# Low halves of some MLP weights by an accumulating DMA instead of a VectorE subtraction

## The chip, the cores and the metric

The kernel runs on one core of a Trainium2 chip. The metric is device time in microseconds (us): the median over the timed runs of the program. A verdict compares two kernels run on the same chip, with a 95% interval.

The core has five engines with instruction queues of their own: TensorE (PE, with its weight loads shown as PEld), VectorE (DVE), ScalarE (ACT), GpSimd (POOL) and SyncE (SP), which here only issues DMAs. The profile numbers the DMA queues: q1 carries what SP issues, q0 what POOL issues; both run on the same 16 DMA engines.

## The reference, cut to what matters

A two-layer decoder trunk over 256 tokens of width 2048, in float32. Layer 0 has a gated short convolution, layer 1 latent attention; both end in an MLP with a hidden width of 8192, followed by a layer norm:

```python
def sq_relu_mlp(x, w1, w2):
    return jnp.square(jax.nn.relu(x @ w1)) @ w2
...
        h = layer_norm(ALPHA * h + sq_relu_mlp(h, mlp_w1[layer], mlp_w2[layer]),
                       ln_g[layer, 1], ln_b[layer, 1])
```

The two MLPs are where the change acts. W1 is 2048 x 8192 and W2 is 8192 x 2048 in each layer.

## The kernel before, in words

**Numbers in two parts.** Matrix products are made in TensorE's fp32r format. To keep float32's accuracy every weight tile is split into a high part, the tile rounded to fp32r, and a low part, what is left over. `split` (L109) does that with two instructions: ACT copies `raw` into `hi` with the rounding (L111), and the DVE subtracts, `lo = raw - hi` (L112). Activations are split likewise, so that a product becomes high by high, high by low and low by high (L190, L194 and `dot`, L245).

**The stream of weights.** All weights are cut into half units, each [128, 1024] in float32, 512 KB. `stream` (L64 to L83) lists them in the order of their use. `take` (L171) hands the next ones to the code that multiplies, and first calls `prepare` (L135) for units up to `LOOK` = 5 ahead. `prepare` loads a unit from HBM on SP's queue (`load_raw`, L130, issue at L132) into one of `RAW` = 5 raw buffers and splits it into a `hi` and a `lo` tile, of which there are `WA` = 8 each (`parts`, L117).

**Who waits for whom.** A load waits for a raw buffer; the buffer is free when the instructions that read it are done. A high part waits for its load and for a `hi` buffer, which is free when PE has used the unit that lies eight back. The low part waits for the high part. No order is written by hand: the framework's scheduler sets the order of each engine's queue when the program is built, from the order of the code and from when it expects an instruction's inputs and buffers to be free. At run time each queue works strictly in that order, so an instruction that waits holds all behind it.

**A pass of an MLP.** The hidden width is worked in `NQ` = 8 passes of 1024 (`mlp`, L523). In each pass:

- W1: eight output tiles of 128 hidden columns, each from two half units, which hold the first and the second 1024 of the contraction (`products`, L230, `mm_run`, L196). In pass 0 these products are made by `mm_wide` (L217) with the layer norm folded in, in passes 1 to 7 by `mm_run`: for each of 16 blocks of the contraction one matmul of 512 columns with the high part (L190) and one of 256 with the low part (L194). The result is evacuated by `whole` (L300: ACT copies one half at L303, the DVE adds the other at L304), goes through ReLU and square on ACT (L562, L563) and is split into `h` (L308, L309).
- Fast W2: in passes 1 to 6 of the first MLP and 1 to 7 of the second (`FAST`, 13 passes in all) the first two of W2's four column blocks are multiplied by a scheme with 7 products instead of 8 (`down_fast`, L287; its matmuls write `ps_f`). Its units, w2f, come in pairs of half units. For each pair the DVE makes a third raw tile, `raw_t`, in a raw buffer (L154), two combinations of half the size (L157, L160), and after three splits a fourth small one, `t` (L162, also through L111 and L112). A pair costs three `hi` and `lo` buffers. Left operands made of `h` stand in `forms` (L566 to L574).
- Plain W2: the other column blocks by `down` (L259; `ps_d`). Results are added into `acc` by the DVE (L546).

**Other users.** POOL has little to do: memsets for the convolution (L507) and for `kpe` (L655), and four loads of the last norm's vectors, `gbt` (L869), at the end of the second MLP.

**Lines that the prediction names.** L111 and L112: the split. L132: the issue of a weight load. L154: the third raw tile of a w2f pair. L190 and L194: high and low matmuls of W1. L247: first matmul of `dot`. L303, L304, L562: evacuation of a W1 product. L869: `gbt`.

Of the kernel before, what the change touches and what calls it, by code (L numbers as in the profile page):

```python
# [9 lines left out]
F32 = mybir.dt.float32  # L10
F32R = mybir.dt.float32r
AF = mybir.ActivationFunctionType
ALU = mybir.AluOpType
# [9 lines left out]
QC = FF // NQ // P  # L23
# [22 lines left out]
def trunk(ctx: ExitStack, tc: tile.TileContext, xT, vecs, w_in, w_out, w_kv, w_q, w_uk, w_uv,  # L46
          w_qn, w_qp, w_o, w1, w2, w2f, cosT, sinT, mask, ident, gb, out):
    nc = tc.nc
# [10 lines left out]
    def halves(w):  # L59

        lead = len(w.shape) - 2
        return [(w,)] if lead == 0 else [h for i in range(w.shape[0]) for h in halves(w[i])]

    stream = []  # L64
# [1 line left out]
        stream += halves(w_in[NC + m]) + halves(w_in[2 * NC + m]) + halves(w_in[m])  # L66
    stream += halves(w_out)

    def mlp_stream(l):
        out = []  # L70
        for q in range(NQ):
            out += halves(w1[l, q * QC:(q + 1) * QC])
            lead = 0
            if q in FAST[l]:
                out += [(w2f[l, q, j, 0], w2f[l, q, j, 1]) for j in range(QC // 2)]
                lead = 2
            out += halves(w2[l, q, lead:])
        return out

    stream += mlp_stream(0) + halves(w_kv) + halves(w_q)  # L80
    for g in range(4):
        stream += halves(w_uk[g]) + halves(w_qn[g]) + halves(w_uv[g]) + halves(w_qp[g])
    stream += halves(w_o) + mlp_stream(1)  # L83

    class Banks:

# [22 lines left out]
    def split(hi, lo, src):  # L109

        nc.scalar.copy(hi, src)  # L111
        nc.vector.tensor_tensor(lo, src, hi.bitcast(F32), ALU.subtract)  # L112

    def tiled(w):
        return w.rearrange("p (b c) -> p b c", c=P)

    def parts(i):  # L117
        return tuple(whl.tile([P, 8, P], F32R, tag=t, name=f"{t}{i}") for t in ("hi", "lo"))
# [11 lines left out]
    def load_raw(i, src):  # L130
        raw = raws.tile([P, 1024], F32, tag="raw", name=f"raw{i}")
        nc.sync.dma_start(raw, src)  # L132
        return raw

    def prepare(i):  # L135

        if len(stream[i]) == 1:
            raw = load_raw(i, stream[i][0])
            hi, lo = ready[i] = parts(i)
            split(hi, lo, tiled(raw))  # L140
            return
        r1, r2 = (load_raw(f"{i}_{j}", src) for j, src in enumerate(stream[i]))
        out = []

        def finished(r, name):
            hi, lo = parts(name)
            split(hi, lo, tiled(r))
            out.append((hi, lo))

        b22, (b21, b12) = r1[:, BW:], (r2[:, :BW], r2[:, BW:])  # L150
        finished(r1, f"{i}_1")
        t = raws.tile([P, 1024], F32, tag="raw", name=f"raw{i}_t")
        two = "p (a c) -> p a c"
        nc.vector.tensor_tensor(t.rearrange(two, a=2), b12.unsqueeze(1).to_broadcast([P, 2, BW]),  # L154
                                r1.rearrange(two, a=2), ALU.subtract)
        finished(t, f"{i}_t")
        nc.vector.tensor_tensor(b12, b22, t[:, :BW], ALU.subtract)  # L157
        finished(r2, f"{i}_2")
        t4 = r1[:, :BW]
        nc.vector.tensor_tensor(t4, b21, b12, ALU.subtract)  # L160
        f = state["fast"].tile([P, 2, BW], F32R, tag="t4", name=f"t4_{i}")
        split(f[:, 0, :], f[:, 1, :], t4)  # L162
        b1, t13, b2 = ([[v.rearrange("p b c -> p (b c)")[:, o:o + BW] for v in w] for o in (0, BW)] for w in out)
        ready[i] = {"11": b1[0], "22": b1[1], "21": b2[0], "T2": b2[1], "T1": t13[0], "T3": t13[1],
                    "T4": [f[:, 0, :], f[:, 1, :]]}
# [5 lines left out]
    def take(halves=2):  # L171

        i = state["next"]
        state["next"] += halves
        ahead = -sum(size(j) for j in range(i, i + halves))
        for j in range(i, len(stream)):
            ahead += size(j)
            if ahead > LOOK:
                break
            if j >= state["split"]:  # L180
                prepare(j)
                state["split"] = j + 1
        return [ready.pop(i + j) for j in range(halves)]
# [295 lines left out]
    for half, cuts in enumerate(FIRST):  # L479
        pieces = [load(2 * u + half, first[:, GROUP * half + u, :], cuts) for u in range(GROUP)]  # L480
        for b0, b1 in zip(cuts, cuts[1:]):
            at = slice(8 * half + b0, 8 * half + b1)
# [502 lines left out]
```

## Time and profile before

| | us |
|---|---|
| median of the two timed runs | 2053.64 (2053.06 and 2054.22) |
| span of the profiled execution, first to last instruction | 2049.4 |
| what lies outside the span, by the difference | 4.2 |
| PE busy | 2030.6 |
| DVE busy | 1662.8 |
| ACT busy | 1194.1 |
| POOL busy | 4.5 |

How to read the profile. A group line gives source line, engine and operation, `out<-in` by the program's tile names, the shape, the count, then busy time, mean of one in ns, and the engine's idle time just before these instructions with what ended it. A line of the timeline gives start, duration, engine, line, operation, tiles, shape and count, and in brackets the idle time before it with its releaser. A row of the windows view gives a stretch in us from the span's start, then the busy time of PE, PEld, DVE, ACT and POOL with instruction counts, the granted clock of TensorE, the mean busy share of the 16 DMA engines, and what they moved in GB/s. A line of the waits view gives who waited for whom, the total, the number of waits and the longest. A DMA issue line gives the queue's engine, the count, the size of one and the median time from issue to landing. Matmuls overlap, so their single durations are longer than their distance.

One pass takes 86.5 us. In the pass that the prediction follows, PE works on W1 from 631.7 to 676.9; its first w2f matmul starts at 676.9.

### The profile page before, as it was taken

What the parts mean: (1) busy time and instruction counts of PE and PEld (TensorE: products, weight loads), DVE (VectorE), ACT (ScalarE), POOL (GpSimd) and SP (SyncE); (2) the same over time, 40 slices, a digit from 0 to 9 for tenths busy, and PEclk for the clock granted to TensorE, in tenths of its full rate; (3) what the DMA queues carried; (4) which work ended last, traced back from release to release, by engine and by line L of the source; (5) the groups of instructions that cost most, each with busy time, mean ns of one, the idle gap of its engine ahead of it and who ended that gap; (6) DMA issues with size and microseconds to landing.
All of it is one profiled execution on the core that took longest, in us unless ns stands there. A gap on an engine that the chain in (4) does not pass through costs nothing.

```text
span 2049.4 us, 30194 instructions
## 1 busy us (share of the span) xinstructions
PE 2030.6 (99%) x11208; PEld 1760.4 (86%) x11208; DVE 1662.8 (81%) x2602; ACT 1194.1 (58%) x1860; POOL 4.5 (0%) x25
## 2 busy tenths in 40 slices
PE   9999999999999999999999999999999999999997
PEld 8888888988888888888889998898888888888885
DVE  7667677678898988989788878776879888898988
ACT  6444445676566565655656665566656656566562
POOL 0000000000000000000000000000000000000000
PEclk9999999999999999999999999999999999999998
DMA  8666666564746557465755544656475664756653
GB/s 308 202 188 187 186 185 194 159 211 136 249 142 223 193 167 250 143 226 173 234 169 164 166 124 142 197 174 196 138 236 161 196 218 156 243 153 217 212 165 137
DMA packets 108003, 385.32 MB, mean 188 GB/s; under 512 B 11984, under 2 KB 13392, under 8 KB 107856
## 3 DMA queue, kind: packets, MB, share of 16 engines
q1 hardware_dynamic: 107136, 381.04, 58.7%
q0 software_dynamic: 576, 2.10, 0.3%
q8 instruction: 88, 1.44, 0.3%
q14 instruction: 59, 0.48, 0.1%
q10 hardware_dynamic: 144, 0.26, 0.0%
HBM read 381.25 MB, written 2.10 MB: 187 GB/s over the span
## 4 chain that ended last, share of the span: by engine, by line
PE 97%; DVE 1%; DMA 1%; issue 0%; ACT 0%; SPq 0%; DVEq 0%
PE ps_u L190 34%; PE ps_u L194 17%; PE ps_d L248 7%; PE ps_d L247 7%; PE ps_d L249 7%; PE ps_f L249 4%; PE ps_f L248 4%; PE ps_f L247 4%; PE ps_w L224 1%; PE ps_w L222 1%; PE ps_w L223 1%; PE ps_g L222 1%; PE ps_g L224 1%; PE ps_g L223 1%; PE ps_wo L190 1%; PE S L788 1%
## 5 line engine op out<-in xcount | busy, mean ns | idle before, releaser
L112 DVE TENSOR_TENSOR lo<-raw,hi 128x1024 fp32r<-128x1024 f32 x712 | 861.7, 1221 | 299.0 <-ACT hi L111 294.3
L111 ACT CAST hi<-raw 128x1024 fp32r<-128x1024 f32 x712 | 742.2, 1049 | 526.6 <-PE ps_u L190 289.5
L190 PE MATMUL ps_u<-xhl,hi 128*128 128x512 f32 x1792 | 632.2, 398 | 0.0
L194 PE MATMUL ps_u<-xhl,lo 128*128 128x256 f32 x1792 | 503.0, 281 | 0.0
L190 PEld LDWEIGHTS ps_u<-xhl,hi 128*128 128x128 f32 x1792 | 336.5, 188 | 82.3
L194 PEld LDWEIGHTS ps_u<-xhl,lo 128*128 128x128 f32 x1792 | 338.5, 189 | 0.5
L190 PE MATMUL ps_u<-xhl_a,hi 128*128 128x512 f32 x720 | 253.4, 396 | 0.0
L248 PE MATMUL ps_d<-lo,h 128*128 128x512 f32 x608 | 236.9, 390 | 0.0
L249 PE MATMUL ps_d<-hi,h 128*128 128x512 f32 x608 | 236.8, 390 | 0.0
L247 PE MATMUL ps_d<-hi,h 128*128 128x512 f32 x608 | 236.6, 389 | 0.0
L194 PE MATMUL ps_u<-xhl_a,lo 128*128 128x256 f32 x720 | 202.9, 282 | 0.0
L190 PEld LDWEIGHTS ps_u<-xhl_a,hi 128*128 128x128 f32 x720 | 135.2, 188 | 31.9
L194 PEld LDWEIGHTS ps_u<-xhl_a,lo 128*128 128x128 f32 x720 | 135.8, 189 | 0.0
L248 PEld LDWEIGHTS ps_d<-lo,h 128*128 128x128 f32 x608 | 114.1, 188 | 24.2 <-DVE lo L112 0.4
L247 PEld LDWEIGHTS ps_d<-hi,h 128*128 128x128 f32 x608 | 114.2, 188 | 24.0
L249 PEld LDWEIGHTS ps_d<-hi,h 128*128 128x128 f32 x608 | 114.1, 188 | 23.9
L111 ACT CAST hi_t<-raw_t 128x1024 fp32r<-128x1024 f32 x52 | 54.8, 1054 | 77.8 <-PE ps_u L190 41.8
L190 PE MATMUL ps_u<-z,hi 128*128 128x512 f32 x256 | 89.0, 392 | 0.0
L562 ACT ACTIVATE fh<-fh 128x256 f32<-128x256 f32 x112 | 46.4, 414 | 72.0 <-DVE fh L304 72.0
L222 PE MATMUL ps_w<-xd,hi 128*128 128x258 f32 x256 | 72.5, 284 | 0.0
L224 PE MATMUL ps_w<-xd,hi 128*128 128x258 f32 x256 | 72.5, 285 | 0.0
L223 PE MATMUL ps_w<-xd,lo 128*128 128x258 f32 x256 | 72.3, 282 | 0.0
(235 smaller groups left out, 3254.8 us busy)
## 6 DMA issues: line engine op xcount, KB each, us to landing
raw<-in_w_dram SPq DMA_DIRECT2D x408, 512.0 KB, 4.4
raw<-in_w2f_dram SPq DMA_DIRECT2D x104, 512.0 KB, 3.6
raw<-in_w_in_dram SPq DMA_DIRECT2D x90, 512.0 KB, 4.2
raw<-in_w_out_dram SPq DMA_DIRECT2D x32, 512.0 KB, 3.6
raw<-in_w_o_dram SPq DMA_DIRECT2D x32, 512.0 KB, 3.9
raw<-in_w_kv_dram SPq DMA_DIRECT2D x10, 512.0 KB, 4.3
raw<-in_w_q_dram SPq DMA_DIRECT2D x8, 512.0 KB, 4.5
raw<-in_w_uk_dram SPq DMA_DIRECT2D x8, 512.0 KB, 4.4
```

What stands on the lines that cost most here:

```text
L111: nc.scalar.copy(hi, src)
L112: nc.vector.tensor_tensor(lo, src, hi.bitcast(F32), ALU.subtract)
L190: nc.tensor.matmul(ps, w[blk // 8][0][:, blk % 8, :], x, start=first, stop=False)
L194: nc.tensor.matmul(ps[:, :T], w[blk // 8][1][:, blk % 8, :], x[:, :T], start=False, stop=last)
L222: nc.tensor.matmul(ps[:, :W], hi, x[k][:, :W], start=k == 0, stop=False)
L223: nc.tensor.matmul(ps[:, :W], lo, x[k][:, :W], start=False, stop=False)
L224: nc.tensor.matmul(ps[:, :W], hi, x[k][:, W:], start=False, stop=k == NC - 1)
L247: nc.tensor.matmul(ps, x[0], w[0], start=first, stop=False)
L248: nc.tensor.matmul(ps, x[0], w[1], start=False, stop=False)
L249: nc.tensor.matmul(ps, x[1], w[0], start=False, stop=last)
L562: nc.scalar.activation(f, f, AF.Relu)
L788: nc.tensor.matmul(S[:, at:at + n], qp[:, tok], kp[:, :n], start=False, stop=True)
```

## The change

For each second half unit of W1 in passes 1 to 7 of both MLPs (8 units a pass, 112 in all) the low part is made in another way. ACT copies the high part as before. ACT then writes its negative into the `lo` tile, an activation with the function Copy and scale -1. Then POOL issues a DMA from the raw tile to the `lo` tile, both in SBUF, that adds to what is there: `lo = -hi + raw`. The DVE instruction at L112 is no longer made for these units. All other units, among them the first halves of the same W1 tiles, all of pass 0, W2 and the attention's weights, are split as before. `summed_lo` holds the places of the changed units in the stream: `mlp_stream` is given the length of the stream so far and notes every second one of a pass's sixteen W1 units.

```diff
+    summed_lo = set()
+
-    def mlp_stream(l):
+    def mlp_stream(l, at):
         out = []
         for q in range(NQ):
+            if q > 0:
+                summed_lo.update(range(at + len(out) + 1, at + len(out) + 2 * QC, 2))
             out += halves(w1[l, q * QC:(q + 1) * QC])
...
-    stream += mlp_stream(0) + halves(w_kv) + halves(w_q)
+    stream += mlp_stream(0, len(stream))
+    stream += halves(w_kv) + halves(w_q)
...
-    stream += halves(w_o) + mlp_stream(1)
+    stream += halves(w_o)
+    stream += mlp_stream(1, len(stream))
...
             hi, lo = ready[i] = parts(i)
-            split(hi, lo, tiled(raw))
+            if i in summed_lo:
+                nc.scalar.copy(hi, tiled(raw))
+                nc.scalar.activation(lo, hi.bitcast(F32), AF.Copy, scale=-1.0)
+                nc.gpsimd.dma_start(lo, tiled(raw), accum_op=ALU.add)
+            else:
+                split(hi, lo, tiled(raw))
             return
```

## The prediction

> **What bounds the kernel now.** I read the page first (busy shares, clock, queues, chain), then the groups by line, then one middle pass of the MLP by windows, waits and timeline.
>
> ```profile
> span 2049.4 us, 30194 instructions
> PE 2030.6 (99%) x11208; PEld 1760.4 (86%) x11208; DVE 1662.8 (81%) x2602; ACT 1194.1 (58%) x1860; POOL 4.5 (0%) x25
> q1 hardware_dynamic: 107136, 381.04, 58.7%
> q0 software_dynamic: 576, 2.10, 0.3%
> PE 97%; DVE 1%; DMA 1%; issue 0%; ACT 0%; SPq 0%; DVEq 0%
> L112 DVE TENSOR_TENSOR lo<-raw,hi 128x1024 fp32r<-128x1024 f32 x712 | 861.7, 1221 | 299.0 <-ACT hi L111 294.3
> L111 ACT CAST hi<-raw 128x1024 fp32r<-128x1024 f32 x712 | 742.2, 1049 | 526.6 <-PE ps_u L190 289.5
> raw<-in_w_dram SPq DMA_DIRECT2D x408, 512.0 KB, 4.4
> raw<-in_w2f_dram SPq DMA_DIRECT2D x104, 512.0 KB, 3.6
> ```
>
> PE is busy for 99% of the span and is 97% of the chain that ended last. Only 18.8 us are open to anyone, so a gain of 2% (41 us, about what a measurement of this kernel can tell from no change) is out of reach unless matmuls themselves get shorter, and the change touches none. The question is whether it makes PE wait.
>
> The stage where it acts is a pass of the MLP. I take pass 3 of the first layer: W1 from 631.7 to 676.9, then the fast w2f units and the plain w2 units. Rows of the windows view (PE, PEld, DVE, ACT, POOL busy, clock, DMA share, GB/s):
>
> ```profile
> 545.20:631.70 86.50, 86.50 (x437) 73.08 (x436) 74.78 (x104) 52.19 (x78) 0.00 (x0) 1.00 0.61 194
> 631.70:676.90 45.20, 45.20 (x257) 39.21 (x256) 38.10 (x59) 28.88 (x49) 0.00 (x0) 1.00 0.55 172
> 617.40:643.10 25.70, 25.70 (x129) 21.72 (x128) 22.09 (x25) 13.95 (x17) 0.00 (x0) 1.00 0.90 303
> 664.00:695.00 31.00, 31.00 (x153) 25.89 (x152) 30.02 (x44) 19.89 (x32) 0.00 (x0) 1.00 0.49 149
> 625.00:630.00 5.00, 5.00 (x24) 4.14 (x23) 4.58 (x5) 3.16 (x3) 0.00 (x0) 1.00 1.00 375
> ```
>
> The clock is full, so nothing there can move. The 16 loads of the pass's W1 units run in a burst (617.4 to 643.1) that fills the DMA engines to 0.90. The DVE is nearly full (30.02 of 31.0) while it prepares the w2f units. Those two places are where slack is short.
>
> **The change part by part.** *DVE loses* 112 subtractions (8 second halves, 7 passes, 2 layers) of 1.22 us: 137 us, or 9.8 us per pass. PE did not wait for them, so this is worth nothing by itself; below it pays back part of a delay.
>
> *ACT gains* 112 negations. Their form, one 128x1024 input written as fp32r, is that of the cast at 1.05 us: 118 us, 8.4 us per pass. In the W1 stage ACT then has 28.9 + 8.4 = 37.3 of 45.2 us. The cover is its idle time, less what it spends waiting for the DVE:
>
> ```profile
> ACT fh L562 <- DVE fh L304: 4.6, 4, 1.4
> ```
>
> That makes 41.9 of 45.2, so I count zero; without the cover each pass loses what exceeds 45.2.
>
> *POOL gains* 112 issues. The only ones in this trace are those of gbt:
>
> ```profile
> L869 POOL DMA_DIRECT2D gbt<-in_gb_dram x4: 527/529/664, 1991.0 to 1992.7; - x4
> DMA to landing us min/median/max: 4.6/5.8/9.4
> ```
>
> At 0.53 us each that is 59 us on an engine with 4.5 us of work; nothing else is queued there in these passes but the memset of kpe and the gbt issues, which already wait until W1 of the last pass is done. A POOL issue waits for ACT's negation, and what queues behind it is only the next accumulation, 5.7 us of PE time later. Zero.
>
> *The DMA engines gain* 112 accumulations of 512 KB that read raw and lo and write lo. No row shows one. From below: as dear as a copy. At a share of 1.00 the engines move 375 GB/s, so 512 KB take 1.40 us of all sixteen (q0's four gbt loads: 0.3% of 2049.4 us over 4, 1.5 us). From above: both reads in full, 2.80 us, if the adder costs nothing; beyond that see the rivals. I take 2.3 us, nearer to the double than to the copy, since the second read is certain and only what a packet pays besides reading can be shared. Over the span q1's loads hold 58.7%, in this pass 0.61 of 86.5 us, so 33.7 us are free and 8 x 2.3 = 18.4 us fit on average. It is not the average that matters.
>
> *Two waits change.* First, the low part of a second half is ready later. Nearest to its use is the first second half of a pass:
>
> ```profile
> 623.60 1.05 ACT L111 CAST hi<-raw 128x1024 fp32r<-128x1024 f32 x1 [1.45 <-DMA raw<-in_w_dram]
> 634.77 0.28 PE L194 MATMUL ps_u<-xhl,lo 128*128 128x256 f32 x1
> ```
>
> High part done at 624.65, negation at 625.7, landing 5.8 + (2.3 - 1.4) = 6.7 us on: 632.4, and PE wants it at 634.8. Zero, with 2.4 us in hand; at the longest landing (9.4 + 1.4) it would be 1.7 us late, 24 us over 14 passes.
>
> Second, the raw buffer stays held until the accumulation has landed, and SP's queue waits for it. Each w2f load waits for such a buffer. The tightest is the one that follows the pass's last W1 unit:
>
> ```profile
> 642.76 0.33 SPq L132 DMA_DIRECT2D raw<-in_w_dram  x1
> ```
> ```profile
> 654.40 1.05 ACT L111 CAST hi<-raw 128x1024 fp32r<-128x1024 f32 x1 [0.58 <-PE ps_u L190]
> ```
> ```profile
> 655.48 1.23 DVE L112 TENSOR_TENSOR lo<-raw,hi 128x1024 fp32r<-128x1024 f32 x1
> 664.01 1.22 DVE L154 TENSOR_TENSOR raw_t<-raw,raw 128x1024 f32<-128x1024 f32 x1
> 690.25 0.68 DVE L112 TENSOR_TENSOR t<-raw,t 128x512 fp32r<-128x512 f32 x1
> ```
> ```profile
> 656.74 0.33 SPq L132 DMA_DIRECT2D raw<-in_w2f_dram  x1
> ```
> ```profile
> 691.55 0.39 PE L247 MATMUL ps_f<-t,h 128*128 128x512 f32 x1
> ```
>
> Before: the unit's load is issued at 642.8, its high part waits for PE until 654.4, the subtraction ends at 656.7 and frees the buffer for the second raw tile of the second w2f unit, which the DVE takes up at 664.0. The DVE's last product for the fourth w2f unit ends at 690.93, and PE uses it at 691.55: 0.6 us in hand.
>
> After, with 2.3 us per accumulation:
> 1. Five accumulations (units 1, 3, 5, 7, 9) fall into the burst, whose idle share is 0.10 x 25.7 = 2.6 us. The last load comes 5 x 2.3 - 2.6 = 8.9 us later: 651.7, landed at 656.1 by the 4.4 us of the page, so the high part is 1.7 us late.
> 2. Two ACT instructions: 654.4 + 1.7 + 2.1 = 658.2. Landing 6.7 us on: 664.9.
> 3. The w2f load takes 3.6 us: 668.5. The DVE is held 4.5 us at 664.0, and all behind it in its queue (evacuations of W1 products, other low parts) too.
> 4. Against it stand the subtraction that is gone (1.2), the DVE's idle time from 664 to 695 (1.0) and the 0.6 us in hand: 4.5 - 2.8 = 1.7 us reach PE.
>
> That happens in the 13 passes that have w2f units (1 to 6 of the first layer, 1 to 7 of the second): 22 us. A stall at the start of a pass would be given back here, so the two are not added. By the same four steps 1.4 us gives 0, 2.1 us gives 6 us, 2.5 us gives 38 us, and 2.8 us gives 61 us. The instruction order is taken from this trace; the scheduler may place a late raw_t differently, which could only shorten step 3.
>
> At the end one real stall exists, and the change could shorten it:
>
> ```profile
> 1993.17 8.60 DMA raw<-in_w2f_dram
> 2001.80 1.23 DVE raw_t L154
> 2008.08 0.55 PE ps_f L248
> ```
>
> The load landed late beside gbt's. It may be issued earlier with a freer DVE or later with a held buffer; I count 0 and keep 4 us either way.
>
> **Sum.** 2049.4 (span) + 22 = 2071.4. The median of the two timed runs, 2053.64, lies 4.2 us above the span, so I forecast 2075.6 us, 1.1% slower: within 2%.
>
> **The rivals.**
> *Hidden wholly.* The accumulation costs the engines 2.0 us or less; the four steps leave nothing for PE. For it: the DMA share is only 0.49 from 664 to 695. Against it: 0.90 in the burst. Time 2050 to 2056, 2053 as its middle. Chance 0.20.
>
> *Two full reads.* The adder fetches both operands at the rate of loads: 2.8 us, 61 us over the 13 passes, 2115 us, slower by 3%. The 2% line is crossed at 2.5 us. For it: both operands must be moved; against it: the 1.40 us row contains HBM, and both tensors here lie in SBUF. Chance 0.18. The Trainium skill, Collectives: The Full Stack, section "The bandwidth ceiling: the fold count and why AG ≠ RS ≠ AR", says that an add in the DMA engine costs no cycles of its own but needs two source reads, and so runs at half the rate of a copy. By that rule the sum would be 2115, not 2076; no run here shows it yet.
>
> *The engines' adder is slow.* Its place is the DMA engines, its price three copies or more. For it: no row speaks against it, and q0's loads landed in up to 9.4 us. Against it: nothing but the size. At 4.2 us (three copies) the free 33.7 us of a pass are used up, and the four steps give 13.1 us per pass: 170 us, 2224 us. It decides, as slower, from 2.5 us on. Chance 0.24.
>
> *ACT becomes the bound of W1.* Its waits on the DVE double to 10 us, since the held DVE delays the evacuations: 47.3 of 45.2 us, 2.1 x 14 = 29 us, 2083 us. Against it: fewer subtractions stand ahead of those evacuations. Chance 0.04.
>
> That the change does not do what it says I give nothing: the indices are the odd ones of the sixteen W1 units, and each is a plain unit.
>
> **How the numbers follow.** Forecast case (2.0 to 2.5 us, 2054 to 2092): 0.33. With hidden 0.20 and ACT 0.04, within 2% is 0.57. Two reads 0.18 and slow adder 0.24 make slower 0.42. Faster by over 2% keeps 0.01, as only 18.8 us are open. The range 2050 to 2200 leaves out the fast edge of the hidden case (0.04) and the larger part of the slow adder (0.15). The forecast's own range is 2054 to 2092.
>
> **What would show it.** Right: q0 at 112 x 2.3 us, some 12 to 13% of the span; ACT about 1312 us and DVE about 1526 us busy; PE waits before ps_f matmuls for DVE t, 1 to 3 us per pass; SP waiting for the accumulation where it waited for DVE lo. Hidden: the same q0 share, and no PE waits. Two reads: q0 near 15% and waits near 5 us per pass. Slow adder: q0 over 23%, loads landing well after 4.4 us, and ACT waiting for raw. Wrong altogether: PE waiting for lo at W1's start, or an order of instructions that has moved.

## The result and the profile after

The changed kernel takes 2185.67 us (2182.79 and 2188.55), the kernel before 2053.64: a ratio of 1.0642, 95% interval [1.0607, 1.0676]. That is 132 us or 6.4% slower, inside the range of 2050 to 2200, but 110 us above the forecast of 2075.6.

The page of the changed kernel (span, engines, the queue q0, releasers on the chain, two groups, and three DMA rows with count, size and median time from issue to landing):

```profile
span 2186.8 us, 30556 instructions
...
PE 2080.7 (95%) x11208; PEld 1780.9 (81%) x11208; DVE 1541.1 (70%) x2490; ACT 1296.3 (59%) x1972; POOL 101.0 (5%) x137
...
q0 software_dynamic: 16704, 60.82, 14.9%
...
PE 59%; DMA 17%; DVE 15%; issue 7%; ACT 2%; DVEq 0%; POOLq 0%; POOL 0%; SPq 0%; ACTq 0%
...
L149 POOL DMA_DIRECT2D lo<-raw x112 | 96.6, 862 | 1724.4 <-ACT lo L148 1257.3
...
L148 ACT ACTIVATE lo<-hi 128x1024 fp32r<-128x1024 f32 x112 | 118.8, 1061 | 1.7
...
raw<-in_w_dram SPq DMA_DIRECT2D x408, 512.0 KB, 4.7
lo<-raw POOLq DMA_DIRECT2D x112, 512.0 KB, 7.2
...
raw<-in_w2f_dram SPq DMA_DIRECT2D x104, 512.0 KB, 3.7
```

PE has fallen from 97% to 59% of the chain: DMA and DVE now stand on it. q0's 14.9% of 2186.8 us, less the 6 us that gbt's loads took before, are 320 us: packet time worth 2.85 us of all 16 engines for one accumulation of 512 KB, 2.04 times the 1.40 us of a load. In the changed kernel L117 and L118 are the old L111 and L112 (the split), L138 is L132 (the issue of a load), L165 is L154 (raw_t), L258 to L260 are L247 to L249 (dot), and L314, L315 and L573 are L303, L304 and L562 (the evacuation); L148 and L149 are the negation and the accumulation.

The waits of the changed kernel (who waited for whom, total, number, longest), then those of SP's queue:

```profile
ACT fh L573 <- DVE fh L315: 135.8, 69, 6.3
...
DVE raw_t L165 <- DMA raw<-in_w2f_dram: 67.1, 13, 6.2
```
```profile
PE ps_f L258 <- DVE fh L315: 43.5, 11, 4.4
PE ps_f L258 <- ACT t L117: 17.9, 13, 2.1
PE ps_f L259 <- DVE t L118: 15.8, 16, 1.4
...
PE ps_u L205 <- DMA lo<-raw: 4.8, 3, 4.1
```
```profile
SPq L138 <- DVE lo L118: 691.7, 293, 12.0
SPq L138 <- DMA lo<-raw: 441.7, 112, 8.4
```

Once in each of the 13 passes that have w2f units, the DVE stands for about 5 us at raw_t, waiting for a w2f load; each time it is the first raw_t of the pass. PE itself waits almost only at the w2f matmuls, for evacuated products (fh) and for the last split (t). In before the DVE's row was 7.6 us and the rows of PE at ps_f came to 2.2 us. SP now waits for an accumulation at every one of the 112 places.

The windows of one pass show why the loads are late: first before, with W1 from 718.2, then after, with W1 from 746.4 (the last but one column is the DMA share):

```profile
718.20:724.20 6.00, 6.00 (x35) 5.18 (x34) 5.38 (x6) 3.41 (x4) 0.00 (x0) 1.00 0.90 299
724.20:730.20 6.00, 6.00 (x36) 5.20 (x35) 3.32 (x5) 3.75 (x7) 0.00 (x0) 1.00 0.86 302
730.20:736.20 6.00, 6.00 (x36) 5.20 (x35) 3.90 (x7) 3.74 (x7) 0.00 (x0) 1.00 0.69 188
736.20:742.20 6.00, 6.00 (x36) 5.21 (x35) 5.29 (x8) 4.38 (x9) 0.00 (x0) 1.00 0.21 77
```
```profile
746.40:752.40 6.00, 6.00 (x36) 5.21 (x35) 2.12 (x3) 1.74 (x2) 0.86 (x1) 1.00 1.05 263
752.40:758.40 6.00, 6.00 (x36) 5.20 (x35) 0.00 (x0) 2.84 (x3) 0.44 (x1) 1.00 1.02 360
758.40:764.40 6.00, 6.00 (x36) 5.21 (x35) 3.83 (x6) 5.97 (x11) 1.28 (x2) 1.00 1.02 257
764.40:770.40 6.00, 6.00 (x36) 5.21 (x35) 3.09 (x7) 3.88 (x7) 0.86 (x1) 1.00 1.01 254
```

In before the burst is over 12 to 18 us into W1. After, the DMA engines are full for 24 us, and the loads that feed the w2f units stand among accumulations.

How one landing sets the next is seen in the pass whose W1 starts at 649.8. These are the DMAs on the chain of work that leads to its first raw_t (start, duration, what):

```profile
643.12 7.68 DMA raw<-in_w_dram
...
653.33 6.79 DMA lo<-raw
...
660.14 7.33 DMA raw<-in_w_dram
...
670.13 7.05 DMA lo<-raw
...
677.20 5.96 DMA raw<-in_w2f_dram
```

A load lands; some 2.5 us later its accumulation is issued, behind ScalarE's copy and negation; when that lands, its raw buffer is free, and SP issues the next load 0.02 us later. Every landing here takes 6 to 8 us, where the loads of before took 4.4 and 3.6 us by the median. The held buffer makes the links, and the full engines make each of them long. In all 13 passes with w2f units the last W1 load and the second w2f load were issued right behind the landing of an accumulation like this.

Where it reaches PE is seen in the same pass. Its timeline, by engine (the row of SP is the pass's last W1 load):

```profile
671.61 0.33 SPq L138 DMA_DIRECT2D raw<-in_w_dram  x1
```
```profile
678.34 1.05 ACT L147 CAST hi<-raw 128x1024 fp32r<-128x1024 f32 x1 [1.45 <-DMA raw<-in_w_dram]
...
685.59 0.42 ACT L573 ACTIVATE fh<-fh 128x256 f32<-128x256 f32 x1 [4.97 <-DVE fh L315]
```
```profile
680.91 0.86 POOL L149 DMA_DIRECT2D lo<-raw  x1 [4.86 <-PE ps_u L201]
```
```profile
683.27 1.22 DVE L165 TENSOR_TENSOR raw_t<-raw,raw 128x1024 f32<-128x1024 f32 x1 [5.09 <-DMA raw<-in_w2f_dram]
...
685.14 0.42 DVE L315 TENSOR_TENSOR fh<-ps_u,t 128x256 f32<-128x256 f32 x1
...
692.18 1.22 DVE L165 TENSOR_TENSOR raw_t<-raw,raw 128x1024 f32<-128x1024 f32 x1
```
```profile
698.90 0.40 PE L260 MATMUL ps_f<-hi_t,forms 128*128 128x512 f32 x1
703.41 0.80 PE L258 MATMUL ps_f<-hi_t,forms 128*128 128x512 f32 x1 [4.11 <-DVE fh L315]
...
709.37 0.63 PE L258 MATMUL ps_f<-hi,h 128*128 128x512 f32 x1
709.80 0.63 PE L259 MATMUL ps_f<-lo,h 128*128 128x512 f32 x1
```

The DVE executes in order: while it stands 5.09 us at the first raw_t, until the load issued at 677.20 has landed, the evacuation behind it waits (685.14), ACT waits for that (4.97), and the products of W1 that the w2f matmuls read are late. The second raw_t (692.18) has no wait of its own: it is late because the DVE is. PE finds the w2f weights of its first matmuls ready, runs on to 698.90 and then stops for 4.5 us. And after that it is slow: 709.37 and 709.80 lie 0.43 us apart, where 0.23 is usual. The windows of this place show the clock:

```profile
690.00:698.90 8.90, 8.90 (x47) 7.52 (x46) 8.75 (x16) 6.39 (x12) 0.00 (x0) 1.00 0.39 119
698.90:703.40 4.50, 0.40 (x2) 0.00 (x0) 4.50 (x7) 2.52 (x5) 0.00 (x0) 0.83 0.00 2
703.40:712.00 8.60, 6.09 (x13) 3.99 (x14) 7.78 (x13) 6.40 (x12) 0.00 (x0) 0.50 0.51 134
```

The stall brings the granted clock down to 0.50 for the next 8.6 us. Taken from the starts of all matmuls, PE stands still for more than 1 us at 41 places, 110.5 us in all (before: 4 places, 5.9 us), and matmuls at the longer distance cost 27.0 us (before 2.7). These two, 104.6 + 24.3 = 129 us, are all but 8 of the 137 us by which the span grew.

### The profile page after: what moved, and what is told of

Read it like the earlier page. It is cut to its first block, busy times and chain, and to the rows that moved or that the text cites. A ratio compares the mean times of both kernels' runs of the same rounds, so it can differ in the third digit from the quotient of the medians.

```text
span 2186.8 us, 30556 instructions
## 1 busy us (share of the span) xinstructions
PE 2080.7 (95%) x11208; PEld 1780.9 (81%) x11208; DVE 1541.1 (70%) x2490; ACT 1296.3 (59%) x1972; POOL 101.0 (5%) x137
## 3 DMA queue, kind: packets, MB, share of 16 engines
q0 software_dynamic: 16704, 60.82, 14.9%
## 4 chain that ended last, share of the span: by engine, by line
PE 59%; DMA 17%; DVE 15%; issue 7%; ACT 2%; DVEq 0%; POOLq 0%; POOL 0%; SPq 0%; ACTq 0%
PE ps_u L201 17%; PE ps_u L205 9%; DMA lo<-raw 8%; DMA raw<-in_w_dram 6%; PE ps_d L259 4%; PE ps_d L260 4%; PE ps_d L258 4%; DVE lo L118 4%; DMA raw<-in_w2f_dram 3%; PE ps_f L259 3%; PE ps_f L260 2%; PE ps_f L258 2%; DVE raw_t L165 2%; DVE lo_t L118 2%; ACT hi L117 1%
## 5 line engine op out<-in xcount | busy, mean ns | idle before, releaser
L118 DVE TENSOR_TENSOR lo<-raw,hi 128x1024 fp32r<-128x1024 f32 x600 | 729.9, 1223 | 371.6 <-ACT hi L117 367.9
L117 ACT CAST hi<-raw 128x1024 fp32r<-128x1024 f32 x600 | 623.0, 1046 | 361.0 <-PE ps_u L201 199.6
L260 PE MATMUL ps_d<-hi,h 128*128 128x512 f32 x608 | 236.7, 389 | 0.0
L258 PE MATMUL ps_d<-hi,h 128*128 128x512 f32 x608 | 236.7, 390 | 0.0
L149 POOL DMA_DIRECT2D lo<-raw x112 | 96.6, 862 | 1724.4 <-ACT lo L148 1257.3
L258 PEld LDWEIGHTS ps_d<-hi,h 128*128 128x128 f32 x608 | 114.2, 188 | 24.0
L260 PEld LDWEIGHTS ps_d<-hi,h 128*128 128x128 f32 x608 | 114.1, 188 | 23.8
L573 ACT ACTIVATE fh<-fh 128x256 f32<-128x256 f32 x112 | 46.2, 413 | 135.8 <-DVE fh L315 135.8
L148 ACT ACTIVATE lo<-hi 128x1024 fp32r<-128x1024 f32 x112 | 118.8, 1061 | 1.7
L165 DVE TENSOR_TENSOR raw_t<-raw,raw 128x1024 f32<-128x1024 f32 x52 | 63.6, 1223 | 67.1 <-DMA raw<-in_w2f_dram 67.1
L201 PE MATMUL ps_u<-z,hi 128*128 128x512 f32 x256 | 90.6, 399 | 0.0
```

Of the source, the lines that this page charges most:

```text
L148: nc.scalar.activation(lo, hi.bitcast(F32), AF.Copy, scale=-1.0)
L149: nc.gpsimd.dma_start(lo, tiled(raw), accum_op=ALU.add)
L201: nc.tensor.matmul(ps, w[blk // 8][0][:, blk % 8, :], x, start=first, stop=False)
L258: nc.tensor.matmul(ps, x[0], w[0], start=first, stop=False)
L260: nc.tensor.matmul(ps, x[1], w[0], start=False, stop=last)
L573: nc.scalar.activation(f, f, AF.Relu)
```

## The experiments

Two theories stood against each other after the result. H, the hold: the accumulation keeps the raw buffer until it has landed, and the burst of W1 loads runs out of its five buffers. D, the DMA time: the accumulation takes so much of the 16 engines that the loads beside it are late. A third was ScalarE's 112 extra passes with the order of instructions that they bring. Ratios are to the kernel before on the same chip, with 95% intervals.

**ScalarE's part alone.**

```diff
-                nc.gpsimd.dma_start(lo, tiled(raw), accum_op=ALU.add)
+                nc.vector.tensor_tensor(lo, tiled(raw), lo.bitcast(F32), ALU.add)
```

> The changed kernel with ScalarE's copy and negation kept and only the accumulating DMA replaced by an addition of raw onto lo on VectorE: same arithmetic, ScalarE has its 112 extra passes of 1.06 us, no DMA and no longer hold than VectorE's reading (one ScalarE pass more than before). Theory of the load burst (held buffers and the accumulations' transfers together make the loss): 2054 to 2065. Rival, ScalarE's extra work and the new order of its instructions are a third factor: 2085 or more, with ScalarE's waits before fh grown from 72 us towards the changed kernel's 136.

Measured 2053.57 us, 0.9998 [0.9989, 1.0008], with ACT busy for 1301.4 us. ScalarE's copy and negation cost nothing; that theory falls, and what is lost comes with the DMA that stands in the place of VectorE's addition. The run says nothing on the lost subtractions, since VectorE makes as many additions (DVE busy 1662.4 us, 1662.8 before).

**The hold alone.** The kernel before, and behind each of the 112 splits three DMAs of 16 columns, each waiting for the one ahead:

```diff
             split(hi, lo, tiled(raw))
+            if i in summed_lo:
+                s = tmp.tile([P, 16], F32, tag="spare", name="spare")
+                nc.gpsimd.dma_start(s, hi.bitcast(F32)[:, 0, :16])
+                nc.gpsimd.dma_start(s, raw[:, :16])
+                nc.gpsimd.dma_start(s, raw[:, 16:32])
```

> The kernel before, with one addition: behind each of the 112 splits POOL issues three DMAs of 16 elements a row onto a small spare tile, one after the other, the first reading hi and the last two reading raw. So raw stays held some 6 to 8 us longer while the DMA engines move almost nothing; lo is still the DVE's. Theory H (the raw buffers, held while an accumulation is under way, pace the loads): 2130 to 2190 us, SP waiting for the small DMAs. Theory D (the time that the accumulations take of the DMA engines): 2050 to 2062 us.

Measured 2190.66 us, 1.0669 [1.0648, 1.0690]. The page's row of q0, SP's wait, the DVE's wait, and a window from the start of a pass's W1 at 749.7:

```profile
q0 software_dynamic: 11328, 4.87, 0.9%
```
```profile
SPq L138 <- DMA spare<-raw: 464.8, 108, 8.6
```
```profile
DVE raw_t L167 <- DMA raw<-in_w2f_dram: 96.9, 25, 9.8
```
```profile
749.70:755.70 6.00, 6.00 (x36) 5.21 (x35) 4.31 (x5) 2.58 (x3) 1.33 (x4) 1.00 0.69 230
```

A hold without bytes, about as long as the accumulation's (SP waits 4.3 us each time, 3.9 in the changed kernel), loses as much as the change, with DMA engines that are 0.69 busy here and 0.60 in the next 6 us. So H alone can do it.

**A short hold.** Only one of the three DMAs is left:

```diff
-                nc.gpsimd.dma_start(s, hi.bitcast(F32)[:, 0, :16])
                 nc.gpsimd.dma_start(s, raw[:, :16])
-                nc.gpsimd.dma_start(s, raw[:, 16:32])
```

> The hold with one small DMA behind each of the 112 splits instead of a chain of three, so that raw is held for one landing of a small DMA behind VectorE's reading and GpSimd never waits for a DMA of its own. If the hold is a cost that grows with its length beyond what the burst has in hand (2.4 us in the prediction): 2053 to 2080, well under the chain's 2190.7. If it is the GpSimd DMA's reading of raw as such, of whatever length (another wait for SyncE on each second load): 2130 or more.

Measured 2051.44 us, 0.9992 [0.9983, 1.0002]. SP still waits for it, 159.0 us at 66 places, and nothing is lost. But this hold is short: GpSimd issues the DMA when the load has landed (110 of the 112 issues waited for that), beside ScalarE's copy, and it lands 3.7 us later by the median, where copy and subtraction take 1.05 + 1.22 us. That keeps the buffer some 1.5 us longer, by an estimate from these figures. So a hold of that length costs nothing, and that a DMA reads raw is not what costs.

**More buffers.** Six raw buffers in the changed kernel, and as a control in the kernel before; to make room, both have one buffer for each of three scratch tags (evac, sq, nu):

```diff
-RAW, WA = 5, 8
+RAW, WA = 6, 8
```

> The changed kernel with six raw buffers instead of five, and three temporary tiles with one buffer less to make room. H: most of the loss goes, 2055 to 2110 us. D: 2175 to 2190 us.

> Control: the kernel before with the same six raw buffers and the same smaller temporaries. Every theory: 2045 to 2058 us.

Measured 2130.20 us, 1.0375 [1.0357, 1.0392], and for the control 2051.71 us, 0.9994 [0.9985, 1.0004]. One buffer takes 55 of the 132 us away: the hold has a real part in the changed kernel too. Then seven, with one fewer for the parts, in both and in the kernel with the hold alone:

```diff
-RAW, WA = 5, 8
+RAW, WA = 7, 7
```

> Control for the next two: the kernel before with seven raw buffers in place of five, and seven of the buffers of high and low parts in place of eight (that is what fits). Before has 1% of PE to lose and nothing of it at the loads, so 2050 to 2060; more than that would be the price of the buffer of parts that is given up.

> The changed kernel with seven raw buffers and seven of parts. One more buffer took the loss from 133 to 77 us. If the hold were all of it, the second more takes it to about 20 to 30 above the control. If the accumulations' transfers cost by themselves what they cost with the buffers free (47 us), it stays 45 to 60 above the control.

Measured: control 2051.88 us, 0.9990 [0.9981, 1.0000]; changed kernel 2133.30 us, 1.0389 [1.0368, 1.0410], 81 us above its control. The second extra buffer brought nothing; both values expected are missed. The hold isn't gone there: SP still waits for an accumulation at 99 places, 416.1 us (five buffers: 112 and 441.7). This kernel also has one buffer fewer for the parts and the same `LOOK` of 5; no run separates these.

> The hold without bytes (three small DMAs behind each of the 112 splits, two of them reading raw) with seven raw buffers and seven of parts. With five buffers it lost 137 us while the DMA engines were 0.37 to 0.83 busy in W1. If the hold costs by too few buffers alone, two more take most of it: 2055 to 2085 beside 2052 for the control. If it still loses 60 or more, then what is left of the changed kernel at seven buffers (81 us) may be hold too, and not the DMA engines' time.

Measured 2117.41 us, 1.0319 [1.0303, 1.0334]: missed as well. This run can't settle the remainder, because its chain has a limit of its own, which its waits show:

```profile
POOL spare L151 <- DMA spare<-raw: 240.0, 96, 5.2
POOL spare L150 <- DMA spare<-hi: 203.3, 102, 5.9
```

With three issues of 0.54 us that is (240.0 + 203.3) / 112 + 1.6 = 5.6 us on POOL per second half, so two units take 5.6 us however many buffers there are, against 3.2 in before's burst. The accumulation has no such waits between its DMAs.

**No hold of raw.** The accumulation reads the weights from HBM once more, so that raw is free after ScalarE's copy:

```diff
-                nc.gpsimd.dma_start(lo, tiled(raw), accum_op=ALU.add)
+                nc.gpsimd.dma_start(lo, tiled(stream[i][0]), accum_op=ALU.add)
```

> The changed kernel with one argument changed: the accumulating DMA reads the unit's weights again from HBM instead of from the raw tile. The accumulations, their bytes on the DMA engines, ACT's negations and POOL's issues stay; only the raw buffer comes free after ACT's copy. Theory H (raw buffers held): 2050 to 2075 us, and SP waits for no accumulation. Theory D (DMA engines' time): 2175 to 2230 us.

> The accumulation that reads the weights from HBM a second time, so that it holds no raw buffer, with seven raw buffers and seven of parts. With five buffers it was 110 us above before. If what is left there is loads that land late beside the transfers, two more buffers cover most of it and the time falls to 10 to 40 us above the control; if it is the DMA engines' time itself or ScalarE's and VectorE's new order, buffers don't help and it stays 80 or more above the control.

Measured 2163.57 us, 1.0532 [1.0516, 1.0548], with five buffers and 2100.43 us, 1.0227 [1.0212, 1.0242], with seven. With five, neither theory's range is met. A window of a pass with five buffers (W1 from 739.5):

```profile
739.50:745.50 6.00, 6.00 (x36) 5.22 (x35) 2.02 (x3) 3.48 (x4) 0.86 (x1) 1.00 1.04 324
```

Without the hold 110 us remain: H is refuted as the only cause. (The 110 us are no exact price, since the second reading from HBM is new too: an accumulation lands 8.5 us after its issue by the median, 7.2 in the changed kernel.) The engines are full, and loads that land later keep a buffer longer by themselves; two more buffers take more than half of it, but not all (expected 10 to 40 above the control, measured 49).

**The traffic alone.** The kernel before, and behind each of the 112 splits an accumulation of 512 KB from hi onto spare tiles, which nobody reads. The first form let ScalarE fill the spares:

> The kernel before, with the traffic added and nothing held: for each of the 112 units ACT writes the negative of hi into two spare half tiles and POOL accumulates hi onto them by two DMAs of 256 KB, the same bytes, ACT time and DMA kind as in the change, but raw is free and lo made by the DVE as before. Three temporary tiles have one buffer less, for room. H: 2050 to 2065 us. D: 2130 to 2190 us. Theory A (ACT's extra 1.06 us a unit): 2100 us or more as well.

Measured 2246.09 us, 1.0941 [1.0923, 1.0960], and inconclusive: ScalarE waited 248.7 us for the spare tiles. Mended, with two spares that no engine fills:

```diff
             split(hi, lo, tiled(raw))
+            if i in summed_lo:
+                for j, s in enumerate(spare):
+                    nc.gpsimd.dma_start(s, hi.bitcast(F32)[:, 4 * j:4 * j + 4, :], accum_op=ALU.add)
```

> The traffic run again without ACT's part, which in e1_traffic had to wait for the spare tiles: the kernel before, with POOL accumulating hi onto two spare half tiles for each of the 112 units, 512 KB a unit. raw is free as before, lo is the DVE's, ACT does nothing new. H: 2050 to 2065 us. D: 2130 to 2190 us.

Measured 2100.62 us, 1.0222 [1.0205, 1.0240]: the traffic costs 47 us, in neither theory's range. It isn't quite alone: the accumulations hold the high parts that they read, and ScalarE waits 18.6 us for them, at 16 places. To see whether it is the bytes or the addition, the same as plain copies, once, twice (j over 0, 1, 0, 1), and once in shorter pieces:

```diff
-                    nc.gpsimd.dma_start(s, hi.bitcast(F32)[:, 4 * j:4 * j + 4, :], accum_op=ALU.add)
+                    nc.gpsimd.dma_start(s, hi[:, 4 * j:4 * j + 4, :])
...
-                    nc.gpsimd.dma_start(s, hi.bitcast(F32)[:, 4 * j:4 * j + 4, :], accum_op=ALU.add)
+                    nc.gpsimd.dma_start(s, hi[:, j::2, :])
```

> The kernel with the accumulations' traffic onto spare tiles (2100.6, raw not held), but each DMA a plain copy of the same 512 KB in place of an accumulation: one read instead of two, 1.4 us of the 16 engines for each unit by before's loads. In W1 of before the engines are 0.9 busy in the first 12 us, so some of it is late, but half the time added: if the engines' time is the cost, 2054 to 2075. If any extra DMA in the burst costs the same, whatever its time: 2090 or more.

> The same with two plain copies of 512 KB for each unit, so that the engines' time is that of the accumulation (about 2.8 us a unit) without any addition. If the DMA engines' time is what costs: 2085 to 2115, like the accumulations' traffic (2100.6). If the accumulating kind does something of its own to the loads beside it: no more than 15 us above the single copy.

> The single plain copy of 512 KB for each unit (2055.5, queue q0 at 9.5%), with the same bytes taken from every second block of 128 numbers, so that the copy goes in shorter pieces and takes the DMA engines longer without any addition. No row shows by how much; the share of q0 will tell. If the engines' time is the cost: with q0 near the 16.3% of the accumulations' traffic, 2085 to 2115; above 16%, more; with q0 still near 10%, no more than 10 us above the single copy, and then the run tells nothing. If only an accumulating DMA harms the loads: at most 10 us above the single copy at any q0.

One copy: 2055.50 us, 1.0016 [1.0006, 1.0025]. Two: 2257.60 us, 1.1004 [1.0986, 1.1022], and inconclusive, because the four DMAs on two spares wait for each other and hold the high parts, and ScalarE waits 188.3 us for them. Pieces: 2064.83 us, 1.0061 [1.0046, 1.0076]. The rows of q0, of the accumulating traffic, of one copy and of the pieces:

```profile
q0 software_dynamic: 32832, 60.83, 16.3%
```
```profile
q0 software_dynamic: 32832, 60.83, 9.5%
```
```profile
q0 software_dynamic: 118848, 60.83, 15.8%
```
```profile
729.40:735.40 6.00, 6.00 (x36) 5.20 (x35) 3.10 (x5) 2.54 (x6) 1.48 (x2) 1.00 1.23 357
```

The same bytes and the same number of DMAs cost 3 to 4 us as copies and 47 as accumulations. So the bytes alone are not what costs, nor that the engines are full for a while: with one copy their share is 1.02 to 1.09 over 18 us of a pass's burst. The held high parts are not the main thing either: ScalarE waits 24.4 us for them in the run with the pieces. Whether it is only the longer time stays open. The copy in pieces has nearly the same share of q0 and costs 12 us, 9 more than one copy; by the value set beforehand (at most 10) that speaks for the accumulating kind. But its window shows a share of 1.23, so packets overlap there and the share says more time than the engines gave.

**Which accumulations hurt.** Only those of the first four W1 tiles of a pass, or only those of the last four (56 units each):

```diff
-                summed_lo.update(range(at + len(out) + 1, at + len(out) + 2 * QC, 2))
+                summed_lo.update(range(at + len(out) + 1, at + len(out) + QC, 2))
...
+                summed_lo.update(range(at + len(out) + QC + 1, at + len(out) + 2 * QC, 2))
```

> The changed kernel with the accumulation on the second halves of W1's tiles 0 to 3 of each pass only, 56 units; tiles 4 to 7 are split by the DVE. H with time to catch up: the loads run ahead again behind the last accumulation, 2055 to 2095 us. Were the loss in proportion to the number, 2120 us. The prediction's step (the pass's last unit holds the w2f load): under 2060 us.

> The reverse: the accumulation on tiles 4 to 7 of each pass only, 56 units. H: as many held buffers, but none behind them to catch up, 2100 to 2165 us. In proportion to the number: 2120 us. The prediction's step (the last unit alone): about 2185 us.

Measured 2126.46 us, 1.0341 [1.0311, 1.0370], and 2086.28 us, 1.0163 [1.0148, 1.0178]. I had the order of the two the wrong way round, and both values of the prediction's step, under 2060 and about 2185, are missed. The early accumulations, which fall into the burst of loads, are the dear ones, although the late ones alone hold a buffer that a w2f load needs next.

One quantity orders nearly all of these runs with five raw buffers: how far into W1 the DVE starts the second raw_t (medians over the 13 passes, from the timelines), beside the median length of the 12 passes that another pass follows:

| kernel | second raw_t, us into W1 | pass, us |
|---|---|---|
| before | 32.3 | 86.5 |
| one small hold | 32.4 | 86.5 |
| one copy | 33.6 | 86.5 |
| copy in pieces | 33.8 | 86.7 |
| last four tiles | 35.6 | 89.0 |
| traffic alone | 36.3 | 90.6 |
| first four tiles | 38.7 | 93.1 |
| from HBM | 41.0 | 95.9 |
| after | 42.9 | 97.9 |
| hold alone | 44.3 | 96.6 |

About 1.3 us are free; beyond that each us of lateness costs 1.0 to 1.5 us of the pass, in most rows more than one, as a stall that takes the clock with it would. The hold alone falls out of the order against the change. The figures don't carry over to seven buffers, where the control starts its second raw_t at 26.2 and the changed kernel at 33.4, with passes of 86.6 and 92.6. Hold and DMA time act on the same thing, the time at which the w2f loads come; that would explain why 137 and 47 us alone are 132 together, but no run shows it by itself.

## Why the prediction was wrong

- *DVE, ACT and POOL by themselves:* right in kind. DVE's busy time fell by 122 us (137 counted), ACT's rose by 102 (118 counted), and POOL's issues took 96.6 us instead of 59. The run with ScalarE's work alone shows that this work did not move the time; no run drops the subtractions alone.
- *The first wait, lo late at W1's start:* right. PE's waits for it sum to 4.8 us, and 4.1 of them are one wait in the middle of W1 in the first MLP's last pass.
- *Size of an accumulation:* mis-sized. 2.3 us was taken, 2.85 measured; the upper bound of 2.80, two full reads, was the right value, and the reason against it (HBM in the 1.40 us) bore nothing. The rule quoted from the Trainium skill, Collectives: The Full Stack, section "The bandwidth ceiling: the fold count and why AG ≠ RS ≠ AR", which states it for collectives, roughly fits: 2.04 times a load, and 1.8 times a copy of the same tiles (traffic alone 16.3% of 2099.7 us, one copy 9.5% of 2053.7, each less 6). The two reads' 2115 us was still 70 too low, so size alone does not mend the sum.
- *Second wait, step 1:* near in number, by luck. The last W1 load was forecast 20.0 us into W1 (11.1 before) and came at 671.61 - 649.8 = 21.8. But the step took the delay from the engines' time alone and put the buffers that the earlier accumulations hold at nothing. That load, like seven others of the pass, was issued when an accumulation had landed; and in the hold without bytes the last W1 load comes as late (20.9 to 26.4).
- *Step 2:* too early. It let that load land in the page's median of 4.4 us and ScalarE follow at once: high part at 24.4. It started at 678.34, 28.5 us in: the load, in full engines, took 6.7 us. The accumulation was issued at 31.1 instead of 26.5.
- *Step 3, the step that failed:* it had the wrong place. It held the DVE at the second raw_t, behind the accumulation of the pass's last W1 unit, and called that load the tightest. The DVE stood at the first raw_t, 5.1 us here and 67.1 us in the 13 passes, behind an earlier accumulation (issued at 670.13, landed at 677.18). At the second raw_t it did not wait at all. That the stand is near the forecast 4.5 us is chance. The first raw_t started 33.5 us into W1 (20.3 before), and so the second at 42.4, not 36.8 (32.3 before): 10.1 us late, not 4.5.
- *Step 4:* it set 2.8 us of saved subtraction, idle time and reserve against 4.5, so that 1.7 reached PE. Measured, this pass became 96.6 us long instead of 86.5, so 10.1 us and not 1.7: 5.6 of the missing 8.4 are the lateness that steps 1 to 3 had too small, 2.8 the reserve. Of the 10.1 us about 7.7 are standstill (gaps of 4.5, 2.05 and 1.87 us, less 0.23 each for the matmul); the rest is the half clock, for which the sum had no term and which takes about what a reserve may have saved. The DVE after its stand is full (8.75 of 8.90 us) and has little to make good with.
- *"The clock is full, so nothing there can move":* wrong. The clock can fall when PE stops. Over the run:

```profile
core 0: 2186.8 us, clock 0.970
```

- *The rivals.* Two reads named the right size and the right sign (q0 near 15%; PE's waits at ps_f, forecast near 5 us per pass, came to 6.4). The slow adder came nearest in time (2224) for a wrong reason: q0 stands at 14.9%, not over 23% (21.5% by its own sum, since 23% divides by the span of before). ACT is not the bound: ScalarE's work alone stays at 2053.57, and in the changed kernel's four windows of W1 ACT is busy for 14.4 of 24 us.

What stays open: how the 132 us divide between hold and DMA time, since each shortens what the other can still take; what keeps 81 us in place with seven buffers, where SP's waits for accumulations go on; and whether an accumulation harms the loads beside it by its time alone.

## What to carry to other kernels

Count first how long an added transfer keeps its source buffer and who is next for that buffer. Here a hold without bytes lost as much as the whole change, and a short one nothing. Judge the transfer in the burst of loads that it falls into, not by the share over the run, and take landing times from full engines there: 6 to 8 us here instead of 4.4. Where loads wait for transfers and transfers for loads, follow the whole loop and not only its last link. Then look at what is queued behind the first instruction, on an engine that executes in order, that waits for a late load. A stall of PE costs more than its length where the granted clock falls with it.

## What the hardware showed unexpectedly

- A DMA that adds costs POOL more to issue: for the same 256 KB from hi to a spare tile 0.88 us (mean of 224 issues in the run with the traffic alone) against 0.53 as a plain copy (mean of 224). The change's own takes 0.86.
- After the stall of 4.5 us the granted clock was 0.50 for the 8.6 us shown. Shorter stalls did it too, but not always. In the run with the traffic alone PE stood for some 2.7 us at several places. At the first of the two shown the clock stayed; behind the second it was 0.50 for 3.4 us.

```profile
689.40:692.20 2.80, 0.56 (x2) 0.24 (x2) 2.80 (x5) 1.56 (x3) 0.00 (x0) 1.00 0.11 16
...
1586.30:1589.10 2.80, 0.56 (x2) 0.25 (x2) 2.80 (x5) 1.57 (x3) 0.00 (x0) 1.00 0.08 12
1589.10:1592.50 3.40, 3.40 (x8) 2.72 (x9) 3.40 (x7) 1.89 (x4) 0.00 (x0) 0.50 0.74 228
```

- With the last four tiles alone, the clock was 0.50 from 867.2 to 870.6 although the longest gap between PE's starts in the 5 us ahead was 1.86 us. So these runs give no length of stall that is safe.
- The Trainium skill, TensorE: Matmul & The Clock Gate, section "Why this matters for your kernels", warns of PE gaps above some 3 us because the clock then drops to half. The stall of 4.5 us agrees with that; the drops behind 2.7 and 1.86 us came below it, and the measurement decides.
- After the stall of 4.5 us the clock stayed low longer than the 3.4 us that the Trainium skill, TensorE: Matmul & The Clock Gate, Part 1, gives for the way back. PE had two more gaps of about 2 us in that time; behind the 2.7 us at 1586.3 it was full again after 3.4 us.
